# The first modulation's products over four 32-wide column tiles

## The chip, the core and the metric

The kernel runs on one core of one Trainium2 chip. Its time is the device time of one execution in microseconds (us); the median of the runs is given. TensorE (PE) multiplies: it first loads a stationary operand (PEld) and then streams a moving one, and writes to PSUM. VectorE (DVE), ScalarE (ACT) and GpSimd (POOL) work element by element, and SyncE (SP) issues the transfers (DMA) from the chip's memory. Each engine works through its own list of instructions in order, and waits on semaphores where it needs another engine's result.

## The reference

The kernel computes two layers of a backbone over 512 latent tokens of 1024 channels and 256 context tokens. Each layer modulates its normalised input by numbers that come from a conditioning vector. The change is in the first two of layer 0's six modulation vectors, shift and scale:

```python
silu_c = jax.nn.silu(c)                                   # (1, 1024)
silu_cc = jax.nn.silu(c_ctx)                              # (1024,)
mod = (silu_c @ w_ada[l] + b_ada[l])[:, None, :]          # 6 x 1024 columns
sh1, sc1, g1, sh2, sc2, g2 = jnp.split(mod, 6, axis=-1)
h = modulate(rms_norm(x, norm1_g[l]), sh1, sc1)           # h * (1 + sc1) + sh1
...                                                       # the same with silu_cc for the context, hc
y, yc = mla_conv_mixer(h, hc, ...)                        # layer 0: h @ a_w_in first, in parts
x = x + g1 * y
x = x + g2 * hier_moe(modulate(rms_norm(x, norm2_g[l]), sh2, sc2), *moe_args)
```

All is float32. The first part of `h @ a_w_in` that the kernel computes is a gated unit: one half of its columns times the sigmoid of the other.

## The kernel before

The program runs in four phases: layer 0's mixer, its experts, layer 1's mixer, its experts. The two expert phases have an order written out by hand. In the mixers a scheduler orders each engine's instructions by its own estimate of their costs, so an edit can move instructions around it.

The change is at the very start, in `attention_mixer` (line 1032). `fetch(t)` (line 1042) issues the loads for step t, t = 0 to 3: two tiles `wada` of 1 MB, one for shift (a=0) and one for scale (a=1), each with 8 chunks c of 128 rows and 256 output columns, and half a megabyte of `wab`, weights of the gated unit. Loads stand on SyncE's queue, and eight counters go round among them: a load waits until the load eight places ahead of it has landed. The order of the loads is: four small tables, two of `X`, then wada, wada, wab of t = 0, wada, wada, wab of t = 1, and so on, then `wb` and others. `X` is normalised on VectorE meanwhile.

`shifts(t)` (line 1052) computes 256 columns of shift and 256 of scale. The stationary operand is `k.sc[:, c, :]`, 128 rows by 32 columns: the two conditioning vectors (tokens and context) after silu, and 30 columns of zeros. The moving operand is a chunk of `wada`. A product therefore uses only 32 of the array's 128 columns, and writes 32 partitions of the PSUM tile `ps_ada`. Line 1057 issues the 16 products: all eight chunks of a=0 into partitions 0 to 31, then all eight of a=1 into partitions 32 to 63. ScalarE copies the 64 partitions to `ada_sb` (line 1059). Two selecting products per call (line 1062) against a 0/1 table `k.sel` turn the rows into columns, VectorE adds the bias (line 1064) and makes the factor `A` (line 1066). Then `mod_T` (line 895) transposes chunks 2t and 2t+1 of `X` on TensorE (line 902, `ps_hT`); ScalarE scales and shifts each into `hxh` (line 906) and VectorE computes the rest `hxl` that float32 needs beyond it (lines 908 and 909). Last, `split` (line 812) cuts `wab` into `wabh` (ScalarE) and `wabl` (VectorE) in the same way.

The mixer's loop calls `shifts(t + 1)` ahead of the products of step t, which go into `ps_glu`: for each of two halves, two parts and two chunks, the three products of `mm3` (lines 806 to 808: high by high, high by low, low by high), 24 a step. After step 3 come the products of the second gated half, `ps_b` and `ps_a`, with `wb` and `wa`, twice 24 each; between them the context `C` is transposed and modulated (`hch`, `hcl`), and then the latent products `ps_lat` with weights `wi`, whose low parts `wil` GpSimd makes.

The later modulations are in `ada` (line 817). There line 826 issues, for each chunk, four products of 512 columns into the four quarters of the partitions, one behind the other:

```python
for j in range(4):
    nc.tensor.matmul(ps[32 * j:32 * j + 32, :], k.sc[:, c, :], w[:, 512 * j:512 * j + 512], ...)
```

Of the kernel before, what the change touches and what calls it, by code (L numbers as in the profile page):

```python
# [8 lines left out]
F32 = mybir.dt.float32  # L9
# [4 lines left out]
OP = mybir.AluOpType  # L14
# [3 lines left out]
P = 128  # L18
# [777 lines left out]
def bank(k, name):  # L796
    return k.psum.tile([P, 512], F32, name=name, tag="ps")
# [13 lines left out]
def split(k, hi, lo, src, eng=None, pin=None):  # L811
    for i in (k.nc.scalar.copy(hi, src), (eng or k.nc.vector).tensor_tensor(lo, src, hi.bitcast(F32), op=OP.subtract)):  # L812
        if pin:
            pin(i)
# [80 lines left out]
def mod_T(k, X, A, s, hp, cs):  # L895

    nc = k.nc
    n = len(X)
    for c in cs:
        ps = bank(k, "ps_hT")  # L900
        for i in range(n):
            nc.tensor.transpose(ps[:, i * P:(i + 1) * P], X[i][:, c * P:(c + 1) * P], k.ident)
        ps = ps[:, 0:n * P]
        a, b = A[:, c, s:s + 1], k.mod[:, 0, c, s:s + 1]
        hi, lo = hp(0, c), hp(1, c)
        nc.scalar.activation(hi, ps, AF.Identity, bias=b, scale=a)
        t = k.work.tile([P, 512], F32, name="mt", tag="w2", bufs=NW2)[:, 0:n * P]
        nc.vector.tensor_scalar(t, hi.bitcast(F32), b, None, op0=OP.subtract)
        nc.vector.scalar_tensor_tensor(lo, ps, a, t, op0=OP.mult, op1=OP.subtract)
# [122 lines left out]
def attention_mixer(k, x, ctx, extra, proj):  # L1032

    nc, q = k.nc, k.q
# [5 lines left out]
    wd, raws = [], []  # L1040
# [11 lines left out]
    def shifts(t):  # L1052

        ps = bank(k, "ps_ada")
        for a in range(2):
            for c in range(8):
                nc.tensor.matmul(ps[32 * a:32 * a + 32, 0:256], k.sc[:, c, :], wd[t][a][:, c, :], start=(c == 0), stop=(c == 7))
        sb = k.work.tile([P, 512], F32, name="ada_sb", tag="w2", bufs=NW2)
        nc.scalar.copy(sb[0:64, 0:256], ps[0:64, 0:256])
        po = bank(k, "ps_ado")  # L1060
        for c in range(2):
            nc.tensor.matmul(po[:, 8 * c:8 * c + 8], sb[0:64, c * P:(c + 1) * P], k.sel[0:64, :], start=True, stop=True)
        for s in range(2):
            nc.vector.tensor_tensor(k.mod[:, :, 2 * t:2 * t + 2, s], po[:, 0:16].rearrange("p (c s a) -> p s a c", s=2, a=4)[:, s, 0:2],
                                    k.bcol(0).rearrange("p (a c) -> p a c", a=2)[:, :, 2 * t:2 * t + 2], op=OP.add)
        nc.vector.scalar_tensor_tensor(A[:, 2 * t:2 * t + 2], k.mod[:, 1, 2 * t:2 * t + 2], 1.0,
                                       k.g1col(0)[:, 2 * t:2 * t + 2, None].to_broadcast([P, 2, 2]), op0=OP.add, op1=OP.mult)
        mod_T(k, X, A, 0, hx, range(2 * t, 2 * t + 2))
        r = raws[t // 2][:, 2 * (t % 2):2 * (t % 2) + 2]
        split(k, w0.t[0][t // 2][:, 2 * (t % 2):2 * (t % 2) + 2], w0.t[1][t // 2][:, 2 * (t % 2):2 * (t % 2) + 2], r)  # L1070
# [10 lines left out]
    fetch(1)  # L1081
    glu = [bank2(k, "ps_glu") for _ in range(2)]
    shifts(0)
    for t in range(4):
        if t < 2:
            fetch(t + 2)
        if t < 3:
            shifts(t + 1)
        if t == 1:
            wb = load_parts(k, [k.w_glu[1]], 8, 256, "wb")  # L1090
        if t == 2:
            Ct = W(k, [P, 2, D], "C")
            nc.sync.dma_start(Ct, ctx.rearrange("(i p) d -> p i d", p=P))
            C = [Ct[:, 0], Ct[:, 1]]
        for s in range(2):
            for m in (1, 0):
                for c in range(2 * t, 2 * t + 2):
                    o = 256 * m + s * P
                    mm3(k, glu[s][:, 512 * m:512 * m + 512], w0(0, c, o, o + P), w0(1, c, o, o + P), hx(0, c), hx(1, c), c == 0, c == 7)
            if t == 3:  # L1100
                unit(s, glu[s][:, 0:512], glu[s][:, 512:1024])
# [497 lines left out]
def body(tc, nc, x, ctx, cc, w_ada, w_ada0, b_ada, norm1, norm2, w_ab, w_glu, w_lat, w_uq, w_ukv, ab_w_out, c_w_in, c_b_in, c_lng, c_lnb, c_wsT,  # L1599
         c_w_out, w_r, w_gu, w_down, const, cols, rowp, out):  # L1600
    es = ExitStack()
    k = K()
# [18 lines left out]
    cst = k.const  # L1621
# [19 lines left out]
    k.tok1 = ct[:, 384:392]  # L1641
    k.tok = ct[:, 694:710].rearrange("p (a q) -> p a q", a=2)
    k.sel, k.ones2 = ct[:, 392:400], ct[:, 400:402]
    k.noff = ct[:, 658:662]
    k.rio = ct[:, 662:694]
    k.cs = ct[:, 402:658].rearrange("p (i f) -> p i f", i=4)
# [225 lines left out]
```

## Time and profile before

| | |
|---|---|
| median of 3 runs | 1419.5 us (1416.41 to 1420.37) |
| profiled execution: its time | 1422.08 us |
| its span, first to last instruction | 1420.3 us |
| TensorE busy in the span | 1223.8 us (86%) |
| VectorE, ScalarE, GpSimd busy | 743.0 (52%), 514.3 (36%), 288.6 us (20%) |
| mean granted TensorE clock | 0.949 of full |
| line 1057's products, first to last start | 16.3 to 59.5 us |

Durations come from this one profiled execution, and times of day in it count from its first instruction. A product's record is its whole passage through the array; products overlap, so a record of 0.38 us can follow the one before by less. A float32 product leaves two records. Rows of a timeline merge consecutive instructions of one line on one engine (x32). [...]

### The profile page before, as it was taken

Reading aid. Unit: us, or ns where it says so; the run is one execution under the profiler, and the core shown is the slowest. Engines: PE = TensorE matmul, PEld = TensorE weight load, DVE = VectorE, ACT = ScalarE, POOL = GpSimd, SP = SyncE. Lnnn points to the kernel's source line nnn. Section 1 sums busy time; section 2 is a strip of 40 time slices with the busy share of each in tenths; the row PEclk is TensorE's granted clock in tenths of the full one; section 3 lists DMA queues with packets and bytes.
Section 4 is the critical chain, followed back from the end, with each engine's and each line's share of the span. In section 5 each row is a group of like instructions: output and inputs, shape, how many; then the busy total and the mean of one; then the engine's idle time right before and its main releaser. Section 6 shows DMA issues by size and latency. Waiting matters only on the chain. (4 is left out here: it accounts for less than half of the span.)

```text
span 1420.3 us, 19799 instructions
## 1 busy us (share of the span) xinstructions
PE 1223.8 (86%) x6894; PEld 793.5 (56%) x6894; DVE 743.0 (52%) x1598; ACT 514.3 (36%) x1235; POOL 288.6 (20%) x270
## 2 busy tenths in 40 slices
PE   5999878899996989989969999999995787777775
PEld 2678654455673444444458898997873333333333
DVE  2334778889567556564684456667346411111116
ACT  3244554476444434333352233335224312211111
POOL 0033455587002011121230001221002100000000
PEclk9999989899997999999989999999997999999998
DMA  9401044726847799989856364453367699988883
GB/s 359 160 29 47 18 155 149 296 72 245 318 157 260 282 365 413 413 347 381 366 179 221 105 231 135 159 172 131 148 237 261 241 365 358 366 342 326 347 325 124
DMA packets 59298, 341.13 MB, mean 240 GB/s; under 512 B 9817, under 2 KB 10073, under 8 KB 24370
## 3 DMA queue, kind: packets, MB, share of 16 engines
q1 hardware_dynamic: 50834, 314.68, 57.1%
q0 software_dynamic: 8224, 23.61, 5.0%
q8 instruction: 106, 1.74, 0.5%
q14 instruction: 134, 1.10, 0.2%
HBM read 321.96 MB, written 21.80 MB: 242 GB/s over the span
## 5 line engine op out<-in xcount | busy, mean ns | idle before, releaser
L357 PE MATMUL mps<-w,xT 128*64 128x512 f32 x1024 | 250.2, 640 | 44.5 <-issue 30.5
L357 PEld LDWEIGHTS mps<-w,xT 128*64 128x64 f32 x1024 | 100.2, 147 | 188.9 <-issue 183.4
L806 PE MATMUL ps_c<-wch,hxh 128*128 128x256 f32 x512 | 147.7, 289 | 2.0 <-ACT hxh L812 2.0
L808 PE MATMUL ps_c<-wch,hxl 128*128 128x256 f32 x512 | 146.0, 286 | 1.5 <-DVE rm_m L98 0.9
L807 PE MATMUL ps_c<-wcl,hxh 128*128 128x256 f32 x512 | 146.2, 286 | 0.0
L363 DVE TENSOR_TENSOR mix<-mix,mps 128x256 f32<-128x256 f32 x32 | 13.5, 421 | 235.0 <-ACT mix L362 235.0
L430 PE MATMUL mps<-w,mix 128*64 128x512 f32 x512 | 116.9, 598 | 8.4 <-ACT mix L371 6.6
L362 ACT ACTIVATE mix<-mps 128x256 f32<-128x256 f32 x32 | 12.3, 384 | 275.1 <-PE mps L357 275.1
L997 POOL TENSOR_TENSOR acc<-acc,ctp 128x497 f32<-128x497 f32 (+14 forms) x71 | 103.1, 1481 | 29.4 <-ACT ctp L996 29.4
L806 PEld LDWEIGHTS ps_c<-wch,hxh 128*128 128x128 f32 x512 | 99.1, 194 | 7.8 <-issue 4.2
L808 PEld LDWEIGHTS ps_c<-wch,hxl 128*128 128x128 f32 x512 | 99.0, 194 | 4.5 <-issue 1.7
L807 PEld LDWEIGHTS ps_c<-wcl,hxh 128*128 128x128 f32 x512 | 99.2, 194 | 4.2 <-issue 3.4
L411 POOL TENSOR_TENSOR X<-X,tmp 128x512 f32<-128x512 f32 x32 | 41.2, 1287 | 203.8 <-ACT tmp L410 180.4
L430 PEld LDWEIGHTS mps<-w,mix 128*64 128x64 f32 x512 | 35.1, 136 | 71.5 <-issue 54.3
L400 PE MATMUL mps<-oy,ooh 128*128 128x512 f32 x272 | 72.7, 408 | 1.7 <-ACTq L729 1.7
L413 DVE TENSOR_TENSOR X<-X,mps 128x512 f32<-128x512 f32 x101 | 64.6, 683 | 5.8 <-PE mps L400 4.9
L806 PE MATMUL ps_o<-woh,yTh 128*128 128x512 f32 x160 | 63.9, 402 | 2.9 <-DVE res L1538 1.7
L807 PE MATMUL ps_o<-wol,yTh 128*128 128x512 f32 x160 | 63.6, 397 | 0.0
L808 PE MATMUL ps_o<-woh,yTl 128*128 128x512 f32 x160 | 62.9, 394 | 0.0
L400 PEld LDWEIGHTS mps<-oy,ooh 128*128 128x128 f32 x272 | 48.5, 189 | 24.9 <-issue 12.1
L812 POOL TENSOR_TENSOR vs<-v,vs 128x512 fp32r<-128x512 f32 x16 | 23.0, 1440 | 182.1 <-ACT vs L812 174.7
L991 DVE SCALAR_TENSOR_TENSOR acc<-z,cl,acc 128x508 f32<-128x508 f32 (+14 forms) x49 | 58.8, 1223 | 0.0
(429 smaller groups left out, 2408.4 us busy)
## 6 DMA issues: line engine op xcount, KB each, us to landing
w<-in_w_gu_dram SPq DMA_DIRECT2D x128, 1024.0 KB
w<-in_w_down_dram SPq DMA_DIRECT2D x64, 1024.0 KB
wada<-in_w_ada_dram SPq DMA_DIRECT2D x48, 1024.0 KB
wc<-in_c_w_in_dram SPq DMA_DIRECT2D x16, 1024.0 KB
wo<-in_c_w_out_dram SPq DMA_DIRECT2D x8, 1024.0 KB
X<-in_x_dram SPq DMA_DIRECT2D x4, 1024.0 KB
wo<-in_ab_w_out_dram SPq DMA_DIRECT2D x4, 1024.0 KB
yd<-zero SPq DMA_DIRECT2D x4, 1024.0 KB
```

The source lines that it names most:

```text
L357: k.nc.tensor.matmul(m.pg[64 * h:64 * h + 64, :], m.xT[:, c, 64 * h:64 * h + 64], st.gu(p, h, c), start=(c == 0), stop=(c == 7))
L363: k.nc.vector.tensor_tensor(m.h, m.sg, m.pg[:, 256:512], op=OP.mult)
L400: k.nc.tensor.matmul(po, self.oh[:, i * P:i * P + P], y[:, 512 * n:512 * n + 512], start=start and y is self.y[0], stop=stop and y is self ...
L411: k.nc.gpsimd.tensor_tensor(X[i][:, c], X[i][:, c], m.tmp, op=OP.add)
L413: k.nc.vector.tensor_tensor(X[i][:, c], X[i][:, c], po, op=OP.add)
L430: nc.tensor.matmul(m.py[n][64 * h:64 * h + 64, :], m.hT[:, f, 64 * h:64 * h + 64], st.dn(p, h, f)[:, 512 * n:512 * n + 512], start=(f == 0 ...
L806: k.nc.tensor.matmul(out, lh, rh, start=start, stop=False)
L807: k.nc.tensor.matmul(out, lh, rl, start=False, stop=False)
L808: k.nc.tensor.matmul(out, ll, rh, start=False, stop=stop)
L812: for i in (k.nc.scalar.copy(hi, src), (eng or k.nc.vector).tensor_tensor(lo, src, hi.bitcast(F32), op=OP.subtract)):
L991: pin(nc.vector.scalar_tensor_tensor(d, zz, w, d, op0=OP.mult, op1=OP.add))
L997: nc.gpsimd.tensor_tensor(d, d, tp, op=OP.add)
```

## The change

The 16 products of a call are issued chunk pair by chunk pair, over four column tiles: tile j = 2a + e takes a = 0 or 1 and the even (e = 0) or odd (e = 1) chunks. Each tile sums four chunks. The copy takes all 128 partitions, and the selecting products, now against `k.sel2`, add the even and the odd sums; `k.sel2` is the sum of neighbouring columns of the old table, made once at the start. The selecting products have 4 columns instead of 8.

```diff
-        for a in range(2):
-            for c in range(8):
-                nc.tensor.matmul(ps[32 * a:32 * a + 32, 0:256], k.sc[:, c, :], wd[t][a][:, c, :], start=(c == 0), stop=(c == 7))
+
+        for c in range(0, 8, 2):
+            for a in range(2):
+                for e in range(2):
+                    j = 2 * a + e
+                    nc.tensor.matmul(ps[32 * j:32 * j + 32, 0:256], k.sc[:, c + e, :], wd[t][a][:, c + e, :], start=(c == 0), stop=(c == 6))
         sb = k.work.tile([P, 512], F32, name="ada_sb", tag="w2", bufs=NW2)
-        nc.scalar.copy(sb[0:64, 0:256], ps[0:64, 0:256])
+        nc.scalar.copy(sb[:, 0:256], ps[:, 0:256])
         po = bank(k, "ps_ado")
         for c in range(2):
-            nc.tensor.matmul(po[:, 8 * c:8 * c + 8], sb[0:64, c * P:(c + 1) * P], k.sel[0:64, :], start=True, stop=True)
+            nc.tensor.matmul(po[:, 4 * c:4 * c + 4], sb[:, c * P:(c + 1) * P], k.sel2, start=True, stop=True)
         for s in range(2):
-            nc.vector.tensor_tensor(k.mod[:, :, 2 * t:2 * t + 2, s], po[:, 0:16].rearrange("p (c s a) -> p s a c", s=2, a=4)[:, s, 0:2],
+            nc.vector.tensor_tensor(k.mod[:, :, 2 * t:2 * t + 2, s], po[:, 0:8].rearrange("p (c s a) -> p s a c", s=2, a=2)[:, s],
...
+    k.sel2 = cst.tile([P, 4], F32, name="sel2")
+    v = k.sel.rearrange("p (j e) -> p j e", e=2)
+    nc.vector.tensor_tensor(k.sel2, v[:, :, 0], v[:, :, 1], op=OP.add)
```

The scheduler answers with another order in the first part of the mixer, up to the first latent products; behind them every engine's list is the same but for line numbers (lines 1060 on stand three, later six lines further down). On TensorE the place is behind call 0's transposes. Before, all of call 1 (two tiles of `wada`, numbered 163 and 164) stands ahead of step 0's first products:

```order
L902 MATMUL ps_hT_204<-ct_68,X_119 128x128 x2
L1057 MATMUL ps_ada_221<-wada_163,sc_88 32x256 x8
L1057 MATMUL ps_ada_221<-wada_164,sc_88 32x256 x8
L806 MATMUL ps_glu_168<-hxh_122,wabh_159 128x512
L807 MATMUL ps_glu_168<-hxl_124,wabh_159 128x512
L808 MATMUL ps_glu_168<-hxh_122,wabl_161 128x512
L1062 MATMUL ps_ado_240<-ct_68,ada_sb_238 128x8 x2
```

In the changed kernel the same place reads (ps_glu 170 and 171 are the two halves of the unit):

```order
L1060 MATMUL ps_ada_223<-wada_165,sc_90 32x256 x2
L806 MATMUL ps_glu_170<-hxh_124,wabh_161 128x512
L807 MATMUL ps_glu_170<-hxl_126,wabh_161 128x512
L806 MATMUL ps_glu_171<-hxh_124,wabh_161 128x512
L807 MATMUL ps_glu_171<-hxl_126,wabh_161 128x512
L808 MATMUL ps_glu_170<-hxh_124,wabl_163 128x512
L806 MATMUL ps_glu_170<-hxh_124,wabh_161 128x512
L808 MATMUL ps_glu_171<-hxh_124,wabl_163 128x512
L806 MATMUL ps_glu_171<-hxh_124,wabh_161 128x512
L807 MATMUL ps_glu_170<-hxl_126,wabh_161 128x512
L808 MATMUL ps_glu_170<-hxh_124,wabl_163 128x512
L1060 MATMUL ps_ada_223<-wada_166,sc_90 32x256 x2
```

Two products of call 1 come first, then ten of step 0's products, of both its chunks, and only then the other fourteen of call 1, in pairs that alternate between the two weight tiles. Calls 2 and 3 are cut in the same way, two and fourteen, with eight and six of step 1's and step 2's products between; eight and thirteen products of the step before stand between those calls' first pair and the transposes ahead of it.

On ScalarE the place is behind step 3, where `ps_b` ends and `wa` is split. Before:

```order
L1075 ACT_TABLE_LOAD
L1075 ACTIVATE sgm<-ps_glu 128x512 x2
L872 ACTIVATE jk,ss<-C 128x1024 x2
L812 CAST wah<-wa 128x1024 x2
L1075 ACTIVATE sgm<-ps_b 128x512
L906 ACTIVATE hch<-ps_hT,mod,A 128x256 x8
L812 CAST wih<-wi 128x672 x3
```

In the changed kernel:

```order
L1078 ACT_TABLE_LOAD
L1078 ACTIVATE sgm<-ps_glu 128x512 x2
L872 ACTIVATE jk,ss<-C 128x1024 x2
L1078 ACTIVATE sgm<-ps_b 128x512
L812 CAST wah<-wa 128x1024 x2
L906 ACTIVATE hch<-ps_hT,mod,A 128x256 x8
L812 CAST wih<-wi 128x672 x4
```

The sigmoid of `ps_b`, which waits for the end of `ps_b`'s products, now stands ahead of the cast that `ps_a`'s products wait for, and four casts of `wi` rather than three stand ahead of the second sigmoid. On TensorE six context transposes rather than two now follow `ps_a`'s first two products, and ten rather than fourteen follow its last.

## Rows read from the trace of the kernel before

**Rows 1.** The page's first line: span and number of instructions.
```profile
span 1420.3 us, 19799 instructions
```
**Rows 2.** Stretches: length, busy us of PE, PEld, DVE, ACT, POOL, clock, DMA, GB/s.
```profile
16.30:25.20 8.90, 8.41 (x33) 3.82 (x33) 3.40 (x8) 1.58 (x3) 0.00 (x0) 1.00 1.03 422
25.20:33.00 7.80, 7.80 (x45) 4.51 (x45) 3.82 (x8) 2.38 (x3) 0.00 (x0) 1.00 1.02 419
40.00:47.00 7.00, 7.00 (x37) 3.57 (x35) 0.00 (x0) 0.37 (x1) 0.00 (x0) 1.00 0.25 102
100.00:177.00 77.00, 67.61 (x394) 60.90 (x393) 42.49 (x116) 33.96 (x98) 34.00 (x48) 0.98 0.09 30
```
**Rows 3.** Timeline of PE: start, length, line, tiles, records [idle before, releaser].
```profile
16.34 8.40 PE L1057 MATMUL ps_ada<-wada,sc 128*32 128x256 f32 x32 [16.34 <-DMA wada<-in_w_ada_dram]
...
26.75 6.26 PE L1057 MATMUL ps_ada<-wada,sc 128*32 128x256 f32 x32
...
39.65 0.39 PE L807 MATMUL ps_glu<-hxl,wabh 128*128 128x512 f32 x1
39.88 0.39 PE L808 MATMUL ps_glu<-hxh,wabl 128*128 128x512 f32 x1
40.20 6.26 PE L1057 MATMUL ps_ada<-wada,sc 128*32 128x256 f32 x32
```
**Rows 4.** Line 1057 by itself: records, ns min/median/max, first and last start.
```profile
L1057 PE MATMUL ps_ada<-wada,sc x128: 379/379/634, 16.3 to 59.5; 128*32 128x256 f32 x128
```
**Rows 5.** Line 826 by itself, and one call's chunk of it on the timeline.
```profile
L826 PE MATMUL ps_ada<-wada,sc x320: 592/617/1063, 197.6 to 961.9; 128*32 128x512 f32 x160
...
203.52 1.07 PE L826 MATMUL ps_ada<-wada,sc 128*32 128x512 f32 x8
```
**Rows 6.** Line 1057 alone in two stretches: PE records, weight loads, clock, DMA.
```profile
28.40:28.90 0.50, 0.50 (x4) 0.22 (x3) 1.00 0.99 410
29.45:29.95 0.50, 0.50 (x7) 0.34 (x7) 1.00 1.20 492
```
**Rows 7.** Timeline of SP's queue: loads issued.
```profile
18.73 1.59 SPq L1046 DMA_DIRECT2D wada<-in_w_ada_dram  x2
...
25.05 0.33 SPq L915 DMA_DIRECT2D wb<-in_w_glu_dram  x1
```
**Rows 8.** Timeline of PE's weight loads in call 0.
```profile
20.15 0.18 PEld L1057 LDWEIGHTS ps_ada<-wada,sc 128*32 128x32 f32 x1 [0.25 <-issue]
20.57 3.68 PEld L1057 LDWEIGHTS ps_ada<-wada,sc 128*32 128x32 f32 x21 [0.25 <-issue]
```
**Rows 9.** Timeline of DVE: the second hxl tile of step 0.
```profile
30.04 0.74 DVE L909 SCALAR_TENSOR_TENSOR hxl<-ps_hT,A,mt 128x512 fp32r<-128x512 f32 x1
```
**Rows 10.** Timeline of ACT, PE and DVE around ps_b's end.
```profile
75.21 1.99 ACT L812 CAST wah<-wa 128x1024 fp32r<-128x1024 f32 x2
77.88 0.39 PE L806 MATMUL ps_a<-hxh,wah 128*128 128x512 f32 x1
78.08 0.60 ACT L1075 ACTIVATE sgm<-ps_b 128x512 f32<-128x512 f32 x1 [0.88 <-PE ps_b L808]
78.39 2.35 DVE L812 TENSOR_TENSOR wal<-wa,wah 128x1024 fp32r<-128x1024 f32 x2
79.66 0.50 PE L808 MATMUL ps_a<-hxh,wal 128*128 128x512 f32 x1 [0.68 <-DVE wal L812]
```
**Rows 11.** Timeline of PE: first context transposes, first product behind them.
```profile
84.81 0.60 PE L902 MATMUL ps_hT<-ct,C 128*128 128x128 f32 x4
...
89.33 0.79 PE L806 MATMUL ps_b<-hxh,wbh 128*128 128x512 f32 x1
```
**Rows 12.** Timeline of PE: a latent product that waits.
```profile
105.96 0.40 PE L807 MATMUL ps_lat<-wil,hch 128*128 128x288 f32 x1 [0.90 <-POOL wil L812]
```
**Rows 13.** Stretches around 89 us, columns as in rows 2.
```profile
85.60:89.00 3.40, 1.77 (x9) 0.87 (x10) 3.30 (x11) 2.92 (x7) 0.00 (x0) 1.00 0.00 0
89.00:92.40 3.40, 3.40 (x9) 2.68 (x10) 2.33 (x7) 2.63 (x5) 1.48 (x1) 0.50 0.02 5
```

## The prediction

> **What bounds the kernel now.** I read the page's span first, then busy time by stretch, then the instructions of the stretch that the change touches. The profiled execution spans 1420.3 us [rows 1]. In the first modulation TensorE is the path: from 16.30 on it is busy 8.41 of 8.90 us, and 7.00 of 7.00 us between 40 and 47 us [rows 2]. Each call of `shifts` holds it for 6.26 us, the first one for 8.40 us [rows 3], and VectorE and ScalarE wait for it meanwhile. Loads do not bind there once the first weights are in: from 40 to 47 us the DMA share is 0.25, and 0.09 from 100 to 177 us [rows 2].
>
> **What the products cost now.** The 64 products leave 128 records, two each, of 0.38 us [rows 4]; 32 of them make the 6.26 us, so they go nearly one after another. The later modulations already go in turn over four column tiles: eight records of 512 columns take 1.07 us, one alone 0.59 to 0.62 us [rows 5]. So four run at once, and a step of four is 1.07 - 0.62 = 0.45 us, or 0.22 us for 256 columns. Different stationary operands do not prevent it: around the turn from a=0 to a=1 seven records of line 1057 touch half a microsecond, where four did before [rows 6].
>
> **Removed, calls 1 to 3.** 32 records over four tiles are eight steps: 7 x 0.22 + 0.38 = 1.92 us in place of 6.26. That is 4.34 us a call, 13.0 us for three, if each step finds its weights. A load waits for the one eight places ahead of it, so the load at 25.05 says that the weights of call 1 are in by then [rows 7]. Ahead of call 2's last tile stand 2.5 MB more, ahead of call 3's 5 MB; at 0.42 MB per us [rows 2] they are in at about 31.5 and 37.5. By the order those calls begin at about 35 and 45 us. No wait there.
>
> **Removed, call 0.** Now its third product needs the second weight tile, which the old order needed only eight products later. That tile is in just before 18.73, when the load waiting for it goes out [rows 7]. TensorE starts the first pair at 16.34, stops, and goes on at 18.8. [...] The new order has a gap. At the half level throughout, it ends at 18.8 + 7 x 0.43 + 0.63 = 22.4, against 24.74 (16.34 + 8.40): 2.3 us earlier. [...]
>
> **Added.**
> - At the half level the selecting products and transposes behind call 0 (26.75 - 24.74 = 2.0 us now, [rows 3]) take longer: none to 1.5 us, taken 0.7.
> - The order puts ten glu products between the first two and the other fourteen products of call 1. They need both hxl tiles; the second is ready at 30.04 + 0.74 = 30.78 [rows 9], 6.0 us after call 0's end [rows 3], which call 1 covered until now. So the fourteen start at 22.4 + 0.7 + 6.0 + 0.5 (two products) = 29.6. Without the wait it would be 22.4 + 2.7 + 0.9 (two products) + 10 x 0.23 = 28.3 [rows 3]: 1.3 us lost. In calls 2 and 3 such products stand behind eight and thirteen of the step before (1.8 and 3.0 us), behind the transposes' 2 us; with the pair and their own first ones that about covers the chain: nothing.
> - If the half level lasts into those ten products and the fourteen, they take 0.20 us more each step: 0 to 3 us, taken 1.0.
> - Calls 1 to 3 now enter and leave the 32-wide form twice: six switches more. Going in costs 40.20 - 39.88 = 0.32 us from start to start, against 0.23 between glu products [rows 3]: 0.09 us each, 0.5 us.
> - ScalarE now does the sigmoid of ps_b ahead of the wah cast. Before, the cast (75.21 to 77.20) was hidden by ps_b's products, and L808 came at 79.66, 1.78 us after they ended [rows 10]. Now it is 0.20 (to the sigmoid) + 0.55 + 1.0 (half the cast) + 1.2 (half of the wal subtraction) = 3.0 us: 1.2 us lost. But four of the fourteen context transposes that took 84.81 to 89.33 [rows 11] now fill that time: 4.5 x 4/14 = 1.3 us back. Net +0.1, between -1.2 and +1.3.
> - The latent products waited 0.90 us for GpSimd's last wil tiles [rows 12]. Four casts rather than three now come ahead of the second sigmoid, so GpSimd starts its fourth tile sooner: 0 to 0.9 us won, taken 0.8.
> - The slow stretch of TensorE's clock at 89 us [rows 13] follows the transposes' gaps, which become fewer; if it goes, half of its 3.4 us is won. From 0 to 1.7 us, taken none.
> - The wider ScalarE copy has as many columns as before, the sum of the selectors (128x4, once, before 5 us) lies beside loads: nothing, at most 0.2 us.
>
> [...]
>
> **Sum.** 2.3 + 13.0 - 0.7 - 1.3 - 1.0 - 0.5 + 0.1 + 0.8 = 12.7 us. Behind the latent products the order on all engines is the same, and loads there start when tiles come free, so the lead should hold to the end. The profiled execution took 1422.08 us (span 1420.3), so by itself it would become 1409.4; the median of the runs, 1419.5, is 2.6 us lower, and I forecast 1419.5 - 12.7, about 1407. Its own range is 1402 to 1412: the better ends above together give 5.4 us more (0.7, 0.7, 1.0, 1.2, 0.1 and 1.7), the worse ones 4.9 less (0.8, 2.0, 1.3 and 0.8).
>
> **Rivals.**
> 1. The half level stays longer. The stretches by clock show it later on: TensorE ran 1.77 of 3.40 us from 85.60 to 89.00, and the next 3.4 us were granted 0.50 [rows 13]. The new gaps up to 30 us are of that kind. Against it: at the half level the work fills the gaps, and before 20.57 gapless work ended in a rise. Two such stretches more, each with about seven steps or products of 0.20 us, plus the 3 us end of the item above: 4 to 6 us lost, 1411 to 1413. [...]
> 2. Half the lead is given back later, because some load behind 177 us is not tied to the work before it: 1413. For it I have only that the DMA queues, nearly idle until 177 [rows 2], carry the experts' weights afterwards; against it, that the order of loads does not change and each waits for a tile that earlier work frees.
> 3. The change does not do what it says: the four tiles do not overlap, since pairs read one moving operand's tile and all four write one bank. Then calls stay at 6.26 us, the switches cost 0.5 and the rest cancels: 1420. Against it stand [rows 5, 6], with one bank and different weights.
> 4. Slower than before: the half level holds through the whole stage, because products now keep coming in short pieces between waits. 96 glu and 24 ps_b products at 0.43 in place of 0.23 us lose 24 us: 1419.5 - 12.7 + 24 = 1431. It decides from 12.7 / 0.20 = 63 products at the half level on. Against it: from 33 us the order is dense, as 7.00 of 7.00 us now.
>
> **Chances.** Forecast 0.65, rival 1 0.17, rival 2 0.08, rival 3 0.05, rival 4 0.05. The range of 8 in 10 is 1402 to 1415: it takes in nearly all of forecast and rival 1 and most of rival 2. A measurement of this kernel tells about 0.3%, 4.3 us, from no change. Faster by more (below 1415.2): 0.87, the forecast, rival 1 and most of 2, less a little for scatter; within: 0.08, rival 3 and tails of 1 and 2; slower: 0.05, rival 4.
>
> **What would show it.** In the changed kernel's rows, a call of 32 records in about 1.9 us instead of 6.26, its records four at a time; call 0 ending near 22.4; a wait of TensorE for hxl near 28 us; the first clock row above or at the half level until about 27; TensorE's wait for the wah cast before L808; the first latent products about 13 us earlier; and the same distance at the end. Wrong would be: calls of more than 4 us (rival 3), many rows at 0.50 before 60 us (rivals 1, 4), or a lead at 100 us that is smaller at 330 (rival 2).

## The result and the profile after

The changed kernel takes 1404.21 us (median of 13 runs, 1392.03 to 1414.18), the kernel before, run beside it, 1416.62 us (13 runs, 1410.44 to 1422.25): ratio 0.9891, 95% interval 0.9868 to 0.9914. The medians are 12.4 us apart; 12.5 was forecast (1419.5 to about 1407), and 1404.2 lies in the range. Its profiled execution took 1409.57 us, so it stands 5 us above its own median. Two of the ten runs of one kernel further down, the one with 126 instructions more and no warming, fell in a slower state; without them its median is 1415.1 us.

The first rows are TensorE's timeline after the change, beside [rows 3]: start, length, line, tiles, records, idle time before.

```profile
15.66 1.07 PE L1060 MATMUL ps_ada<-wada,sc 128*32 128x256 f32 x4 [15.66 <-DMA wada<-in_w_ada_dram]
18.02 3.63 PE L1060 MATMUL ps_ada<-wada,sc 128*32 128x256 f32 x28 [1.29 <-DMA wada<-in_w_ada_dram]
...
24.87 1.07 PE L1060 MATMUL ps_ada<-wada,sc 128*32 128x256 f32 x4
26.74 0.79 PE L806 MATMUL ps_glu<-hxh,wabh 128*128 128x512 f32 x1 [0.80 <-ACT wabh L812]
...
31.08 1.92 PE L1060 MATMUL ps_ada<-wada,sc 128*32 128x256 f32 x28
...
37.65 0.62 PE L1060 MATMUL ps_ada<-wada,sc 128*32 128x256 f32 x4
38.20 0.50 PE L806 MATMUL ps_glu<-hxh,wabh 128*128 128x512 f32 x1
...
40.24 1.92 PE L1060 MATMUL ps_ada<-wada,sc 128*32 128x256 f32 x28
42.09 0.51 PE L806 MATMUL ps_glu<-hxh,wabh 128*128 128x512 f32 x1
...
69.43 0.50 PE L806 MATMUL ps_a<-hxh,wah 128*128 128x512 f32 x1 [1.62 <-ACT wah L812]
```

Call 0 ends at 18.02 + 3.63 = 21.65 (before: 24.74). Each later call stands in two pieces: four records, whose next product starts 0.55 us later (37.65 to 38.20), and 28 records, 1.85 us (40.24 to 42.09). The glu products wait at 26.74, for ScalarE's cast of their weights.

The stretches, beside [rows 2, 13]: length, busy us of PE, PEld, DVE, ACT, POOL, clock, DMA share, GB/s.

```profile
17.90:21.70 3.80, 3.63 (x28) 1.36 (x28) 2.54 (x4) 0.00 (x1) 0.00 (x0) 1.00 1.01 425
31.00:60.00 29.00, 29.00 (x206) 20.97 (x206) 12.78 (x25) 9.24 (x13) 0.00 (x0) 1.00 0.59 222
71.70:75.10 3.40, 3.40 (x9) 2.63 (x9) 2.90 (x7) 0.47 (x2) 0.00 (x0) 0.50 0.46 103
```

From 31 to 60 us TensorE never waits. The stretch at half level (granted clock 0.50) that stood at 89 us is now at 71.7.

A mark for the lead is the first latent product on hxh, whose order has not changed; the rows give first and last start of its group, in the profile before and after.

```profile
L806 PE MATMUL ps_lat<-wih,hxh x64: 288/334/440, 110.3 to 144.2; 128*128 128x288 f32 x32, 128*128 128x384 f32 x32
```
```profile
L806 PE MATMUL ps_lat<-wih,hxh x64: 288/334/522, 99.2 to 134.7; 128*128 128x288 f32 x32, 128*128 128x384 f32 x32
L807 PE MATMUL ps_lat<-wil,hch x16: 294/295/298, 92.2 to 98.2; 128*128 128x288 f32 x16
```

The lead there is 110.3 - 99.2 = 11.1 us. None of these 16 latent products on hch passes 298 ns and none waits now: the 0.90 us for GpSimd [rows 12] are gone.

### The profile page after: what moved, and what is told of

The parts are those of the page before. It is cut to its first block, busy times and chain, and to the rows that moved or that the text cites. A ratio compares the mean times of both kernels' runs of the same rounds, so it can differ in the third digit from the quotient of the medians.

```text
span 1407.8 us, 19802 instructions
## 1 busy us (share of the span) xinstructions
PE 1214.5 (86%) x6894; PEld 788.7 (56%) x6894; DVE 745.5 (53%) x1599; ACT 513.8 (36%) x1235; POOL 288.4 (20%) x270
## 5 line engine op out<-in xcount | busy, mean ns | idle before, releaser
L808 PE MATMUL ps_c<-wch,hxl 128*128 128x256 f32 x512 | 145.8, 285 | 1.5 <-DVE rm_m L98 0.9
L363 DVE TENSOR_TENSOR mix<-mix,mps 128x256 f32<-128x256 f32 x32 | 13.5, 421 | 234.3 <-ACT mix L362 234.3
L997 POOL TENSOR_TENSOR acc<-acc,ctp 128x497 f32<-128x497 f32 (+14 forms) x71 | 103.2, 1481 | 29.6 <-ACT ctp L996 29.6
L808 PEld LDWEIGHTS ps_c<-wch,hxl 128*128 128x128 f32 x512 | 98.8, 193 | 4.5 <-issue 1.7
L400 PEld LDWEIGHTS mps<-oy,ooh 128*128 128x128 f32 x272 | 49.9, 193 | 25.5 <-issue 11.7
L808 PE MATMUL ps_o<-woh,yTl 128*128 128x512 f32 x160 | 62.9, 394 | 0.0
```

Source lines behind the costliest of these rows:

```text
L400: k.nc.tensor.matmul(po, self.oh[:, i * P:i * P + P], y[:, 512 * n:512 * n + 512], start=start and y is self.y[0], stop=stop and y is self ...
L808: k.nc.tensor.matmul(out, ll, rh, start=False, stop=stop)
L997: nc.gpsimd.tensor_tensor(d, d, tp, op=OP.add)
```

## The experiments

The table gives for each kernel the median, the ratio to the kernel before with its 95% interval, the mark from the same row as above, and the lead (110.3 less the mark).

| kernel | median us (runs) | ratio | mark | lead |
|---|---|---|---|---|
| changed | 1404.21 (13) | 0.9891 (0.9868 to 0.9914) | 99.2 | 11.1 |
| tiles one after another | 1409.88 (8) | 0.9958 (0.9926 to 0.9989) | 105.0 | 5.3 |
| two tiles in turn | 1411.0 (10) | 0.9954 (0.9919 to 0.9990) | 103.4 | 6.9 |
| warm | 1416.21 (10) | 0.9991 (0.9958 to 1.0025) | 93.7 | 16.6 |
| wah cast first | 1406.03 (6) | 0.9919 (0.9885 to 0.9953) | 100.8 | 9.5 |
| calls kept whole | 1398.75 (4) | 0.9880 (0.9832 to 0.9929) | 94.5 | 15.8 |
| warm, 254 instructions more | 1400.17 (6) | 0.9888 (0.9854 to 0.9922) | 94.9 | 15.4 |
| 126 instructions more, not warm | 1416.66 (10) | 0.9996 (0.9959 to 1.0034) | 94.9 | 15.4 |
| warm, 254 more, calls whole | 1394.79 (4) | 0.9856 (0.9800 to 0.9912) | 93.7 | 16.6 |
| changed, second and third profile | 1403.94, 1412.27 (1 each) | | 97.0, 97.1 | 13.3, 13.2 |
| before, second profile | 1416.84 (1) | | 108.7 | 1.6 |

**Tiles one after another.**
```diff
-for c in range(0, 8, 2):
-    for a in range(2):
-        for e in range(2):
+for a in range(2):
+    for e in range(2):
+        for c in range(0, 8, 2):
```


> Even and odd weight rows still go to four column tiles, but one tile's four products are issued before the next tile's. Theory (the gain comes from four tiles at work at the same time): 32 records of a call again take nearly one after another, 5 to 6.3 us in place of 1.92, so the first latent products lose 11 us or more of their lead and stand within 2 us of the kernel before; time about 1416, ratio to before 0.998 to 1.003. Rival (the gain comes from the moved glu products and casts, or from the narrower selecting product): the calls are longer but the lead of 11 us at 105 us stays above 6 us, time below 1410. A call of about 1.9 us with the tiles in blocks would say that the issue order does not matter.

TensorE's timeline in this kernel, half of call 1 and the product behind it:

```profile
24.74 2.81 PE L1060 MATMUL ps_ada<-wada,sc 128*32 128x256 f32 x16
27.48 0.50 PE L806 MATMUL ps_glu<-hxh,wabh 128*128 128x512 f32 x1
```

A call takes 2 x 2.74 = 5.48 us, as the theory has it, but the lead is 5.3 us, where at most 2 were expected, and the median of 1409.9 us lies where the rival put it (below 1410). The lead nearly adds up (5.7 us) from things that are not the turn: call 0 ends 1.9 us earlier (1.0 of that because its first load landed at 15.38 rather than 16.34), three calls are 0.7 us shorter each (6.19 before, 40.20 [rows 3] to 46.39, the next product's start; an estimate of the cause: a call has four groups of records with edges instead of two, and at such an edge [rows 6] show seven records in half a microsecond, four elsewhere), and this execution had no slow stretch before the mark (1.7 us). What the changed kernel has beyond this, calls of 2.40 in place of 5.48 us, is the turn.

**Two tiles in turn, in the kernel before.**
```diff
-        for a in range(2):
-            for c in range(8):
+        for c in range(8):
+            for a in range(2):
```


> The kernel before, with its two column tiles in turn (row c of both shifts, then row c+1) and everything else as it was. Theory (n tiles in turn take 1/n of the time): 16 steps of two records at 0.22 us, 15 x 0.22 + 0.38 = 3.7 us a call in place of 6.26, and call 0 as early as in the four-tile kernel or 1 us later; lead at the first latent products 13 x 2.6 / 4.34 = 7.8 us from calls 1 to 3, less the same waits as with four tiles: 5 to 8 us, ratio 0.994 to 0.997. Rival (four tiles are needed, since two leave the time of a record bound by its weights): call above 5 us, lead below 3 us. Other rival (the lead is bound by the chain behind call 0, not by the length of the calls): lead 10 to 11 us, as with four tiles.

TensorE's timeline, call 2:

```profile
40.09 3.65 PE L1057 MATMUL ps_ada<-wada,sc 128*32 128x256 f32 x32
```

3.65 us a call and a lead of 6.9 us: both rivals fall. One, two and four tiles at work make 6.26, 3.65 and 1.92 us.

**A warm TensorE.** Products of ones whose result nobody reads.
```diff
...
+    warm(57)          # 128x128 by 512 columns, bf16
...
+                if t == 0 and c == 0 and a == 1:
+                    warm(6, k.tc.keep_in_program_order)
```


> The changed kernel with 57 products of ones by ones (bf16, 512 columns, a bank that nobody reads) ahead of call 0, and six more between call 0's first two weight tiles, so that TensorE has no gap there. Theory (call 0, its selecting products and the ten glu products of call 1 are slow because TensorE stood idle ahead of them): granted clock 1.00 from 16 us or a little later, call 0's last 28 records in about 2 us in place of 3.63, glu products 0.23 in place of 0.43 us apart; the first latent products 2.5 to 4 us earlier than in the changed kernel. Rival (the wait for the hxl tiles bounds this stretch, so a faster TensorE only waits longer): clock 1.00, but latent products earlier by 1.5 us or less. Third way (the half level comes at another place instead, as the stretches after 60 us moved): same lead within 0.7 us at 105 us.

The time is that of the kernel before. TensorE's timeline: call 0's last records, and the products behind two of the jumps between the last experts (PEq is TensorE's sequencer).

```profile
18.30 1.92 PE L1069 MATMUL ps_ada<-wada,sc 128*32 128x256 f32 x28
...
1195.21 8.54 PE L357 MATMUL mps<-w,xT 128*64 128x512 f32 x32 [3.01 <-PEq L486]
...
1324.10 8.78 PE L357 MATMUL mps<-w,xT 128*64 128x512 f32 x32 [3.05 <-PEq L486]
```

The same two jumps on the timeline of the changed kernel:

```profile
1203.65 7.09 PE L357 MATMUL mps<-w,xT 128*64 128x512 f32 x32 [1.20 <-PEq L486]
...
1316.32 8.78 PE L357 MATMUL mps<-w,xT 128*64 128x512 f32 x32 [2.28 <-PEq L486]
```

The stretch from 1150 to 1350 us of the warm kernel (columns as above):

```profile
1150.00:1350.00 200.00, 150.35 (x666) 57.93 (x662) 28.23 (x56) 32.50 (x136) 13.70 (x14) 0.91 0.78 313
```

and of the changed kernel:

```profile
1150.00:1350.00 200.00, 156.52 (x743) 66.13 (x741) 32.21 (x64) 39.01 (x164) 15.65 (x16) 0.96 0.88 352
```

The code that was brought in between the first of these jumps and the next one (queue q8, taken to be that of TensorE's code; packets, MB, share), in the warm kernel from 1196.5 to 1237 us:

```profile
q8 instruction: 4, 0.07, 0.8%
```

and in the changed kernel from 1204 to 1241.5 us:

```profile
q8 instruction: 4, 0.07, 0.6%
```

Up to the mark the theory holds: call 0's last 28 records take 1.92 us, and the lead is 16.6 us, 5.5 more than in the changed kernel's first profile and 3.3 more than in its repeated ones (further down), which have a slow stretch ahead of the mark that this one lacks. But the same product starts 8.4 us ahead of the changed kernel's at 1195.21, and 7.8 us behind it at 1324.10. No theory had that. The engine waits 2.9 to 3.3 us at each of four jumps, where the changed kernel waits 1.20 at three and 2.28 at the last, and the products behind such a wait are slower too: 8.54 us for the 32 records at 1195.21, 7.09 in the changed kernel. The clock in this stage is 0.91 instead of 0.96, and the loads move 313 instead of 352 GB/s; that they only follow a late TensorE is not shown.

As many code packets come from one jump to the next, four in both kernels; what differs is when. Ahead of each long wait here, the packet starts 0.8 to 0.9 us before the products of line 459, TensorE's last work ahead of the jump, end. Ahead of the waits of 1.2 us it starts at least 3.2 us before that. In all profiles together, the waits of 1.8 us and more at the last five such jumps end 3.5 to 4.1 us after the start of such a packet, the changed kernel's last one included (1.84 us before, wait 2.28). The new theory: the 63 products move the code behind them, and a jump's code now comes too late to be hidden behind work.

**The first cast of wah ahead of the sigmoid, as before.**
```diff
...
+            with k.tc.issue_after(wai[2].ins):
+                unit(2, pa, pb)
```


> The changed kernel with ScalarE's first sigmoid of the second glu part issued behind the third wah cast, as it stood in the kernel before; no other change of what is computed. Theory (the order of these two costs a wait that context transposes only partly fill): TensorE's wait of 1.62 us for wah ahead of the product at 69.43 becomes 0.7 us or less, and the stretch at half level at 71.5 us goes, so latent products 1 to 3 us earlier than in the changed kernel. Rival (the transposes fill the time, as the prediction had it with +0.1 net): latent products within 0.7 us of the changed kernel's.

TensorE's timeline behind ps_b's last product:

```profile
69.27 0.30 PE L902 MATMUL ps_hT<-ct,C 128*128 128x128 f32 x1 [1.43 <-issue]
69.88 0.55 PE L902 MATMUL ps_hT<-ct,C 128*128 128x128 f32 x3 [0.31 <-DVE C L880]
71.01 0.66 PE L808 MATMUL ps_a<-hxh,wal 128*128 128x512 f32 x1 [0.59 <-DVE wal L812]
```

The wait for wah is gone, but 1.43 + 0.31 + 0.59 us of others stand in its place, and L808 comes at 71.01 in place of 71.46, where the first load landed 0.34 us earlier anyway. Up to that product the rival holds: the order is worth 0.1 us. Half level stays at 71.2 us (products 0.43 us apart there, 0.23 behind it). The mark itself comes 1.6 us later than in the changed kernel, outside both expectations, with a further stretch at half level at 81.4 us (0.43 us again); whether the order brings that stretch is not shown.

**Calls kept whole.**
```diff
+        last.append(mm)       # the call's last product
...
+          with k.tc.issue_after(last[-1].ins):   # the glu products
```


> The changed kernel with the glu products of one step issued only behind the last of the next call's sixteen products, so that no call is cut in two and the six switches fall away. Theory (the first-modulation products wait for the hxl tiles only because ten glu products stand inside call 1; by the prediction that is 1.3 us of wait and 0.5 us of switches): call 1 runs in one piece at half level from about 24.9 to 28.5, the glu products follow behind it, and the first latent products come 1 to 3 us earlier than in the changed kernel. Rival (without the call's products to fill in, the chain of norm, casts and transposes behind call 0 sets when the next glu products start, so the cut costs nothing): latent products within 0.7 us of the changed kernel's.

TensorE's timeline: call 2 in one piece, and a latent product:

```profile
33.65 1.93 PE L1060 MATMUL ps_ada<-wada,sc 128*32 128x256 f32 x32
35.51 0.50 PE L806 MATMUL ps_glu<-hxh,wabh 128*128 128x512 f32 x1
...
90.14 0.40 PE L807 MATMUL ps_lat<-wil,hch 128*128 128x288 f32 x1 [0.91 <-POOL wil L812]
```

A whole call takes 1.86 us to the next product (33.65 to 35.51; call 1, at 23.46, takes 2.38), a cut one 0.55 + 1.85: the fourteen products behind the cut still give two of the tiles their full eight records, so what is taken out ahead shortens nothing. The lead is 15.8 us. Against the repeated profiles of the changed kernel below, which also had full level from 22 us and one slow stretch ahead of the mark, it is 2.5 us more, 0.5 of that by the first load (15.47 for 16.04 and 15.92); the wait for GpSimd's tile is back, 0.91 us. The 2.0 us that are left lie within the 1 to 3 of the theory.

**The warm kernel moved on by 254 instructions.** 73 products of 32 columns and 48 of 512 stand ahead of call 0, where the warm kernel has 57 of 512; with the six inside call 0, that is 254 instructions more on TensorE than in the changed kernel, in the warm kernel 126 more.
```diff
-    warm(57)
+    for i in range(73):       # four column tiles in turn, 32 columns each
+        j = i % 4
+        nc.tensor.matmul(wm[32 * j:32 * j + 32, 0:32], k.ones_bf[:, 0:32], k.ones_bf[:, 0:32], ...)
+    warm(48)
```


> [...] Theory (the earlier one lost its lead at the end because its jumps between the last experts found their code in another block: waits of 3.0 us where 1.2 us stood): the waits behind L459 from 1150 us on are 1.2 us again, the lead of 16 to 17 us at 105 us holds to the end within 4 us, and the time is 1394 to 1402. Rival (the warm engine itself, by starting the later stages earlier or by using up its clock, brings the half level into the experts' stage): waits or slow stretches there as in the earlier warm kernel, time 1409 to 1418.

TensorE's timeline behind the same jump:

```profile
1193.16 7.09 PE L357 MATMUL mps<-w,xT 128*64 128x512 f32 x32 [1.20 <-PEq L486]
```

The stretch of the last experts:

```profile
1150.00:1350.00 200.00, 154.70 (x752) 66.87 (x748) 32.19 (x64) 39.09 (x164) 16.61 (x17) 0.98 0.91 363
```

The waits are 1.2 us again, all four, and the loads run at 363 GB/s. The time is as expected, and the lead, rather than holding, grows from 15.4 to 25 us at 1385 us; that the second profile of before also stands 5 us earlier there explains part of it, the rest stays open. A warm engine does no harm there. Between the profiles of the two warm kernels, the four waits differ by 7.4 us in sum (12.2 and 4.8) and the 32 records behind each of them by 6.1 us (34.6 and 28.5): 13.5 us, where these profiles are 23.8 apart and the medians 16.0. So more than half of the difference stands at these jumps, as the theory has it; the rest was not traced. That code lies in blocks is the theory's guess; the runs show packets of 16 KB (4 make 0.07 MB).

**Only the shift: 126 instructions, no warming.**
```diff
...
+    for i in range(63):
+        j = i % 4
+        nc.tensor.matmul(wm[32 * j:32 * j + 32, 0:32], k.ones_bf[:, 0:32], k.ones_bf[:, 0:32], ...)
```


> The changed kernel with 63 products of 32 columns of ones (a bank that nobody reads) ahead of everything, 126 instructions more on TensorE, done by 4 us and with no work between them and call 0. Theory (the place of the code decides what jumps cost at the end): call 0 at half level and the lead of 9 to 11 us at 105 us as in the changed kernel, but waits of about 3 us behind L459 from 1190 us on, and 8 to 16 us lost there: 1412 to 1420. Rival (the early start or the clock did it): same jumps of 1.2 us and same time as the changed kernel, 1400 to 1408.

TensorE's timeline behind the same jump:

```profile
1190.56 9.86 PE L357 MATMUL mps<-w,xT 128*64 128x512 f32 x32 [3.24 <-PEq L486]
```

0.7 us of small products at the start cost 11 us at the end (1415.1 us against the changed kernel's 1404.2). The theory on the code's place holds: 63 products make all four waits long, with and without warming, and 127 do not, though in the next kernel, also with 127, the last jump waits 3.71 us. The lead of 15.4 us was not expected: in this execution full level came at about 22 us and no slow stretch stood ahead of the mark.

**Warm, 254 instructions, calls whole.** The products of ones and the order of the two experiments together.
```diff
+    warm(48)                                     # behind the 73 narrow ones
...
+          with k.tc.issue_after(last[-1].ins):   # the glu products
```


> The warm kernel with 254 instructions more, and the glu products of a step behind the next call's last product, so that no call is cut. If warming up and keeping the calls whole each win time, latent products come 1 to 3 us earlier than in the warm kernel alone, time 1392 to 1400; if the calls' cut only fills a wait that stands there anyway, the same within 0.7 us at the latent products.

The lowest median of all (runs from 1390.16 to 1399.85), though its interval overlaps that of the changed kernel. TensorE's timeline, a latent product:

```profile
89.41 0.40 PE L807 MATMUL ps_lat<-wil,hch 128*128 128x288 f32 x1 [0.90 <-POOL wil L812]
```

The lead is 16.6 us, 1.2 more than the 15.4 of the warm kernel with 254 instructions more, within the 1 to 3 expected, although the wait for GpSimd is back.

**The same kernels again, for more profiles.** No edit.

> The changed kernel once more, unchanged, for a second profile. Theory (when the half level behind call 0 ends is decided by how the execution falls, not by the order of the work): this or the next one shows full level by about 22 us, as two kernels with the same rows up to there did, and then a lead at the latent products of 14 to 16 us in place of 11; time below 1403 then. Rival (the order of the changed kernel itself keeps the level low): glu products 0.43 us apart until about 30 us in both, lead 10 to 12 us.

> The changed kernel a third time; theories and numbers as for the second: half level to about 30 us and a lead of 10 to 12 us, or to about 22 us and a lead of 14 to 16 us.

> The kernel before once more, unchanged. Theory (stretches of half level fall in different places from one execution to the next): the stretch at 89 us is gone or elsewhere, call 0 takes 7.4 to 13.6 us by the level it meets, the first latent products stand 1 to 4 us from where they stood at 106 us. Rival (they belong to the order of the work): call 0 8.4 us long with the rise at 20.6, a stretch at 88 to 90 us, latent products within 0.7 us.

TensorE's timeline in the changed kernel's second profile:

```profile
18.41 3.54 PE L1060 MATMUL ps_ada<-wada,sc 128*32 128x256 f32 x28 [1.30 <-DMA wada<-in_w_ada_dram]
22.43 0.61 PE L1065 MATMUL ps_ado<-sel,ada_sb 128*128 128x4 f32 x4 [0.47 <-ACT ada_sb L1062]
...
26.03 0.50 PE L806 MATMUL ps_glu<-hxh,wabh 128*128 128x512 f32 x1 [1.51 <-ACT wabh L812]
...
28.94 1.92 PE L1060 MATMUL ps_ada<-wada,sc 128*32 128x256 f32 x28
```

ScalarE's cast and VectorE's two hxl tiles ahead of these products, in the same profile:

```profile
24.94 2.00 ACT L812 CAST wabh<-wab 128x1024 fp32r<-128x1024 f32 x2
25.02 0.75 DVE L909 SCALAR_TENSOR_TENSOR hxl<-ps_hT,A,mt 128x512 fp32r<-128x512 f32 x1
...
27.21 0.75 DVE L909 SCALAR_TENSOR_TENSOR hxl<-ps_hT,A,mt 128x512 fp32r<-128x512 f32 x1
```

The level rises at about 22 us in both, so its end at 30 us in the first profile belonged to that execution. Of the five profiles with this order up to there, it came at 30 us in two (the first, and that of the wah cast). The lead is 13.3 and 13.2 us, not 14 to 16, and neither time is below 1403: a slow stretch at 69.5 us (granted clock 0.50) stayed. The two agree to 500 us and end 8.3 us apart. Their mean granted clocks, 0.950 and 0.947, account for about 4.5 us of that by estimate (1410.5 x 0.003 / 0.950); the rest was not traced. In the kernel before, call 0 took 8.17 us, a stretch stood at 87.3, and the mark came at 108.7: 1.6 us earlier, of which its first load explains 1.2 (landed 15.14 in place of 16.34). That leaves 0.4 us, so the rival is nearer, and the stretch stands behind the same transposes in both executions.

## Why the prediction came out as it did, step by step

The gain is near the forecast because terms that were off cancel. The step that failed is the price of calls 1 to 3: 12.5 us by the prediction (13.0 less 0.5 for switches), 11.4 measured.

- **Four tiles at once: right.** 32 records in 1.92 us, as worked out; rival 3 is dead. The experiments with one and two tiles at work show that it is the turn.
- **Call 0, +2.3: right.** It ends 3.1 us earlier, 0.7 of that by the load (15.66 for 16.34), which leaves 2.4. The 0.43 us a step is the distance of the weight loads in [rows 8] before 20.57 us, 0.18 behind it; ahead of the first clock entry, "half level" stands for that spacing. The first 0.7 of the range's better end stands for a rise of the level halfway through the call, as before; no run of this kernel shows it: the last 28 records take 3.63, 3.54 and 3.62 us in its three profiles, 1.92 at full level.
- **Calls 1 to 3 and "six switches more", 13.0 - 0.5: too large by 1.1.** The step "4.34 us a call" failed: a cut call holds TensorE for 0.55 + 1.85 = 2.40 us, where 6.19 stood from start to next start, so 3 x 3.79 = 11.4. The prediction gave the cut only two switches of 0.09 us, but the piece behind it is as long as a whole call. No run here separates the switch from the cut; both together cost 0.54 us a call (2.40 less 1.86).
- **The wait ahead of call 1's fourteen, -1.3: right in kind, 0.5 short, wrong in the releaser.** At full level the products wait 1.51 us for wabh and 0.29 more for wabl, 1.8 in all. The first glu product starts when the first half of wabh is cast, 26.0 us in the second profile, 0.2 us after the first hxl. The second hxl, the tile that the prediction named, is ready at 27.96, 6.0 us after call 0's end as forecast, but only the ninth of the ten products needs it, and that one starts at 28.38. By this tile alone the fourteen could have started at about 28.5. They start at 31.08 or 28.94, forecast 29.6. That calls 2 and 3 wait for nothing was right (busy 29.00 of 29.00 us from 31 to 60).
- **Half level, -0.7 and -1.0: -2.5 in one profile, 0 in two.** From the first load to the fourteen products it is 15.42 us in the first and 12.90 in the second. The end of the half level was not to be had from the order: in three executions of one program it came at 21.7, 21.8 and 30.8 us, 9 us apart; why was not traced. It is rival 1's first half, at a price of 2.5 us in one of three executions.
- **Order of the wah cast, +0.1; the wil wait, +0.8; the slow stretch, 0: right.** Measured 0.1 lost, 0.9 won, and a stretch at 69 to 72 for one at 87 to 89.
- **What would show it: one sign wrong.** The clock's rows say 1.00 over 17.9 to 21.7 us, where 28 records take 3.63 us in place of 1.92. The trace has no clock entry ahead of the first rise (30.8 us in this profile), so that 1.00 is no reading, and the first half level shows in the spacing of products only.
- **The sum.** With the measured terms 2.4 + 11.4 - 1.8 - 2.5 - 0.1 + 0.9 = 10.3, and 0.7 for the load: 11.0 us, against a lead of 11.1. (This profile waits only 0.80 us for wabh; the 2.5 us are what its half level adds beyond the 1.8.) For the second profile 2.4 + 11.4 - 1.8 - 0.1 + 0.9 + 0.3 = 13.1, against 13.3. Over all profiles of the two kernels the mark stands at 97.8 (99.2, 97.0, 97.1) for 109.5 (110.3, 108.7): 11.7 us, forecast 12.7. A cut and a wait priced too low, and a half level priced as if it always came, nearly cancel, so that the total is near is in part luck.
- **"The lead should hold to the end": not shown for single executions.** Behind the mark TensorE's products are the same in the same order, so one of them can be followed. The last group of six transposes ahead of 331 us starts as follows, in the first and second profile of before and the first of the changed kernel:

```profile
330.12 0.82 PE L1266 MATMUL ps_pT<-ct,pr 128*128 128x128 f32 x6
325.72 0.82 PE L1266 MATMUL ps_pT<-ct,pr 128*128 128x128 f32 x6
319.68 0.82 PE L1269 MATMUL ps_pT<-ct,pr 128*128 128x128 f32 x6
```

In the first pair the lead of 11.1 us is still 10.4 there. Over all five profiles (the second and third of the changed kernel have 320.23 and 320.27) the means are 7.9 us apart, where 11.7 stood at the mark, and their spans end 10.8 us apart. The prediction took a lead that is smaller at 330 us for a sign of rival 2. But the kernel before alone moves by 4.4 us there from one execution to the other, where 1.6 stood at the mark, so five profiles can't tell whether something is given back. What is firm is the 12.4 us between the medians of 13 runs each. The changed kernel has as many instructions on TensorE as the one before, a condition that the prediction did not name: with 126 more, the gain was gone (ratio 0.9996), with an order as unchanged as here. Rival 2 looked at loads; here four jumps wait 2.66 to 3.24 us in place of 1.20 at three and 2.28 at the last.

## What to carry to other kernels

Column tiles paid here where products of different tiles follow one another (32 records in 1.92 us, in 5.48 one tile after another), and a group cut in two kept the length of its longest tile's chain (1.85 us for the fourteen products behind the cut, 1.86 for all sixteen): keep such a group whole. Before a gain is credited to an edit that adds or drops instructions, look at the waits behind jumps far down the program: they moved the time as much as the edit did (11 to 16 us, the edit 12.4). Where TensorE has just stood idle, price the length of the half level as something that differs between executions (here it ended at 22 or 30 us; with products of ones ahead, call 0's 28 records took 1.92 us at once), and judge small steps by a mark close behind the edit, over several profiles.

## What the runs showed of the hardware

- **The place of the code.** 126 instructions at the start made four jumps 1200 us later wait 2.7 to 3.3 us in place of mostly 1.2, and cost 11 to 16 us; 254 cost nothing in the warm kernel (four waits of 1.19 to 1.21 us, median 1400.2). As many code packets of 16 KB (4 make 0.07 MB) come either way; at the long waits they come later. Other shifts were not tried, nor was it traced why the packet of the changed kernel's own last jump comes later (waits of 2.28 to 3.07 us, where 1.39 and 1.85 stood before).
- **One, two, four tiles** take 6.26, 3.65 and 1.92 us for 32 records, with one PSUM bank and a weight load for each record.
- **Half level ahead of the first clock entry**, seen in the spacing of products only (0.43 us at half level, 0.23 at full), and its end at 22 or 30 us in the same program.
